# Two mixer blocks and their experts on one core: the token mixer's two branches in the other order, RWKV's two directions in turn, and eight extra weight slots for the first expert

## The chip, the core and the metric

The kernel runs on one core of a Trainium2 chip. TensorE (PE) multiplies matrices, VectorE (DVE), ScalarE (ACT) and GpSimd (POOL) do the elementwise work, and SyncE (SP) issues nearly all weight transfers. The metric is the device time of one execution in microseconds. Each engine runs its own instructions in order, so what stands in what place of an engine's row is a part of the design.

## What is computed

Two transformer blocks follow each other. The first has 16 meta tokens and 256 tokens (272 rows of 1024); the second works on the 256 tokens and on a context of 256.

```
# block 1
u    = rmsnorm(h);  rq, rk, rv, rg, mq, mk, mv, mo, gates = split(u @ w_in)
ret  = retention(rq, rk, rv), forward + backward;  y_ret = head_norm(ret) * silu(rg)
mq, mk = silu(conv5(mq, mk))
hm   = sigmoid(mo) * (mlstm(mq, mk, mv, gates), forward + backward);  y_m = head_norm(hm)
h   += concat(y_ret, y_m) @ w_out
aff  = softmax(rmsnorm(h) @ w_router);  16 experts take their 34 best tokens each
h   += sum over experts of  w_down(silu(w_gate x) * (w_up x)) * aff      # d_ff 2816
# block 2, on the tokens, with states that the context leaves
cols = u @ w_in_2;  o_a = gated_delta(cols_a), two directions;  o_b = rwkv7(cols_b), two directions
h   += merge(sigmoid gates, o_a, o_b) ;  h += two-level MoE(h), 32 experts
return rmsnorm(h)
```

Retention and mLSTM don't depend on one another; both go into the one product with `w_out`. The two directions of the RWKV scan don't depend on one another either; their results are added.

## The kernel before

**The head** (`head_body`, from L399) computes block 1's mixer. Every projection is a set of three fp32r products (`product3`, L299: high times high, high times low, low times high) whose weights come by `wgroup`. The order in which the code is written is: retention's q and k (`rqk`), retention's scores (`rs`), its values, its sums (`ro`, `head_norm`); then mLSTM's q and k, values and gates, its scores (`ms`, L616) and sums (`mo`, L639) head by head, each sum evicted through a small chain on ACT and DVE (`rc`, L642 to L647); then the output gate, a head norm (`y<-hnmv`, L733), and the projection `gate` of retention. Afterwards `y` is transposed in eight pieces k (`trb`, L680), four of retention (with `gate`, L684) and four of mLSTM, split into high and low parts, and multiplied with `w_out` (`pM`, L395, for the meta rows, then `wo`). Between these stand small steps of block 2's conditioning (`ada`). `route` then does the softmax and, in some 20 small steps on DVE, the choice of tokens (`af`, `wk`, `gt`, `eq`, `ce`).

**The experts** (`ffn`, L820). Weights arrive in slots of 1 MB, taken in turn (`Ring`) from three pools of ten slots together; for expert 0 a pool `rx` with four further slots stands on the right side of the memory, in the ring behind the ten. SP issues the transfers in one row (L241 for `w_gate` and `w_up`, L283 for `w_down`, L265 for the context's `w_in_2`), and each waits until the tiles that lay at its slot's place are done with. An expert's weights are 34.6 MB. `expert` (L883) computes gate and up products (`gu`, L901) and `second` (L917) the down product (`dn`, L933). From expert 1 on, the context's share of block 2 (`ctx_pre`) is placed between these products.

**RWKV** (L1414) takes its 8 heads in four pairs j. For each pair and each direction d there is a front (`rwkv_front`: products `rmt`, L1628), an inverse (`mixed_inverse`: many 32x32 products `r0ic`, `r1ic`, L1164, then `r1ib`, `r1iy`), and a scan of four steps (`rwkv_back`: `rp`). A step is a chain: `T` times state (L1661, which waits for the state `rSU`), copy on ACT, product with `Y` (L1676), copies on DVE and ACT, update (L1683), the new `rSU` on DVE (L1688); L1691 adds the step's output. Before, `rwkv_back` is run to its end for direction 0 and then for direction 1. The projections of what comes later (`pc`, L1102, and `gz`, L1836) are placed behind instructions of direction 0 (`hop`, `fill`). The delta-rule branch (`gic`, `gib`, `gp`) and these projections share the stretch with RWKV.

What sets the order: the code is written in one order, and a scheduler that plans with a timeline of its own then orders every engine's instructions; on the chip each engine runs them in that order and waits where an operand is missing.

Of the kernel before, what the change touches and what calls it, by code (L numbers as in the profile page):

```python
# [10 lines left out]
F32 = mybir.dt.float32  # L11
# [5 lines left out]
P = 128  # L17
D = 1024
KD = D // P
# [36 lines left out]
RX = 4  # L56
# [106 lines left out]
class Net:  # L163
# [237 lines left out]
    def head_body(self, W):  # L401
# [9 lines left out]
        wq = self.wgroup(w_in, 0)  # L411
# [6 lines left out]
        for q in (64, 96):  # L418
            nc.gpsimd.tensor_add(self.fold4, self.fold4, self.ident[:, q:q + NMETA])

# [21 lines left out]
        for hh in range(4):  # L442
            s = rvt(hh, f"strip{hh}")[:, :416] if hh < 3 else W.tile([P, 416], F32, name="strip3", tag="mv0", padded_shape=[P, 516])
# [13 lines left out]
        rqk = []  # L457
        for g in range(2):
            dst = W.tile([P, 4, NTOK], F32, name="qk", bufs=4)
            scale = (P ** -0.5) if g == 0 else 1.0  # L460
            for j in range(4):
                if j % 2 == 0:
                    w = wq if g + j == 0 else self.wgroup(w_in, 512 * g + 128 * j)
                    if g:
                        step(g)
                pj = projT(w, j % 2)
                raw = W.tile([P, NTOK], F32, name="raw", tag="raw", padded_shape=[P, NTOK + 4], bufs=3)
                nc.scalar.activation(raw, pj, AF.Copy, scale=scale)
                tmp = W.tile([P, NTOK], F32, name="rtmp", tag="rtmp", bufs=2)
                for i in (0, 64):  # L470
                    a, c = slice(i, i + 64), slice(64 - i, 128 - i)
                    nc.vector.scalar_tensor_tensor(tmp[a], pj[c], scale, self.ht("sin")[c], op0=ALU.mult, op1=ALU.mult)
                nc.gpsimd.tensor_mul(dst[:, j, :], raw, self.ht("cos"))
                nc.vector.tensor_add(dst[:, j, :], dst[:, j, :], tmp)
            rqk.append(dst)

        big = W.tile([P, 4, 3, NTOK], F32, name="pret", tag="big")
        prets = [big[:, hh] for hh in range(4)]
        self.ptag = "pc"
        for hh in range(4):  # L480
            pret = prets[hh]
            for t, (n0, n) in enumerate(TT):
                b = self.bank("rs")
                nc.tensor.matmul(b[:n, :NTOK], rqk[1][:, hh, n0:n0 + n], rqk[0][:, hh, :], start=True, stop=True)
                nc.vector.tensor_mul(pret[:n, t, :], b[:n, :NTOK], strip[hh][:n, 144 - n0:416 - n0])
# [3 lines left out]
        rv = [rvt(t, f"rv{t}") for t in range(3)]  # L489
# [24 lines left out]

        projN(1024, out_rv)


        self.ptag = "pc"
        for t, (n0, n) in enumerate(TT):
            ro = self.bank("ro")  # L520
            for hh in range(4):
                for m, (m0, mn) in enumerate(TT):
                    nc.tensor.matmul(ro[:n, hh * P:(hh + 1) * P], prets[hh][:mn, m, n0:n0 + n],
                                     rv[m][:mn, hh * P:(hh + 1) * P], start=(m == 0), stop=(m == 2))
            self.head_norm(W, y[:n, t, 0:512], ro[:n], n, f"r{t}")


        self.ptag = "pa"
        mqk = []
        for g in range(2):  # L530
            dst = W.tile([P, 4, NTOK], F32, name="qk", bufs=4)
            for j in range(4):
                if j % 2 == 0:
                    w = self.wgroup(w_in, 2048 + g * 512 + 128 * j)
                    step(1)
                pj = projT(w, j % 2)
                pad = W.tile([P, NTOK + 4], F32, name="pad", tag="raw", bufs=3)
# [1745 lines left out]
```

## Time and profile before

| | |
|---|---|
| median of 3 runs | 2490.26 us (2485.04 to 2493.68) |
| profiled execution | 2486.04 us |
| its span, first to last instruction | 2484.3 us |
| TensorE busy | 2306.2 us, 93% of the span |
| mean granted TensorE clock | 0.965 of full speed |
| VectorE, ScalarE, GpSimd busy | 40%, 26%, 14% |
| transferred | 755.06 MB, mean 304 GB/s |

The span falls into the head (0 to some 268 us), the routing (to 293 us), the sixteen experts (to some 1668 us), block 2's mixer (to some 2200 us) and its MoE. The profile shows for each engine what it did and what ended its idle time; a stretch's own numbers say more than the means of the span, since the stages have different limits.

### The profile page before, as it was taken

Reading aid. Unit: us, or ns where it says so; the run is one execution under the profiler, and the core shown is the slowest. Engines: PE = TensorE matmul, PEld = TensorE weight load, DVE = VectorE, ACT = ScalarE, POOL = GpSimd, SP = SyncE. Lnnn points to the kernel's source line nnn. Section 1 sums busy time; section 2 is a strip of 40 time slices with the busy share of each in tenths; the row PEclk is TensorE's granted clock in tenths of the full one; section 3 lists DMA queues with packets and bytes.
Section 4 is the critical chain, followed back from the end, with each engine's and each line's share of the span. In section 5 each row is a group of like instructions: output and inputs, shape, how many; then the busy total and the mean of one; then the engine's idle time right before and its main releaser. Section 6 shows DMA issues by size and latency. Waiting matters only on the chain. (4 is left out here: it accounts for less than half of the span.)

```text
span 2484.3 us, 45165 instructions
## 1 busy us (share of the span) xinstructions
PE 2306.2 (93%) x18736; PEld 1252.2 (50%) x18736; DVE 990.8 (40%) x2419; ACT 656.0 (26%) x1652; POOL 350.8 (14%) x627
## 2 busy tenths in 40 slices
PE   7997799999999999899999998978998999989997
PEld 6765433444444434333433333327777777865554
DVE  6655311323332133223133133216566563645545
ACT  4443111211211222111122121114534332522221
POOL 3101100000001111101011011004243231300000
PEclk9998899999999999999999999998997889999999
DMA  7664999999999999999999999992311113689995
GB/s 244 225 233 132 336 407 402 402 407 405 400 407 398 361 402 405 406 408 406 406 400 406 406 406 406 408 354 67 88 37 38 45 27 95 224 278 365 367 367 182
DMA packets 318816, 755.06 MB, mean 304 GB/s; under 512 B 12944, under 2 KB 158016, under 8 KB 315536
## 3 DMA queue, kind: packets, MB, share of 16 engines
q1 hardware_dynamic: 317104, 747.67, 80.3%
q0 software_dynamic: 1504, 4.46, 0.6%
q8 instruction: 150, 2.46, 0.4%
q14 instruction: 58, 0.48, 0.1%
HBM read 751.03 MB, written 1.05 MB: 303 GB/s over the span
## 5 line engine op out<-in xcount | busy, mean ns | idle before, releaser
L901 PE MATMUL gu<-w,xs 128*64 128x512 f32 (+1 forms) x3072 | 677.2, 568 | 24.3 <-DMA w<-in_w_up 17.2
L901 PEld LDWEIGHTS gu<-w,xs 128*64 128x64 f32 x3072 | 197.5, 137 | 325.2 <-issue 258.0
L933 PE MATMUL dn<-w,hT 128*64 128x512 f32 x1408 | 338.1, 604 | 17.0 <-DMA w<-in_w_down 16.9
L1102 PE MATMUL pc<-luT,w 128*128 128x256 f32 x688 | 177.5, 398 | 1.8 <-DMA w<-in_w_in 1.8
L933 PEld LDWEIGHTS dn<-w,hT 128*64 128x64 f32 x1408 | 88.4, 136 | 171.7 <-issue 116.7
L1102 PEld LDWEIGHTS pc<-luT,w 128*128 128x128 f32 x688 | 126.6, 195 | 19.2 <-DMA w<-in_w_in 2.0
L2139 PE MATMUL egu<-w,exs 128*64 128x256 f32 x1024 | 123.2, 383 | 0.0
L2139 PEld LDWEIGHTS egu<-w,exs 128*64 128x64 f32 x1024 | 74.6, 136 | 39.4 <-issue 6.9
L1672 POOL TENSOR_SCALAR rsw<-rSU,rwc 64x64 f32<-64x64 f32 x112 | 37.2, 332 | 389.3 <-DVE rSU L1688 379.0
L911 DVE TENSOR_TENSOR hid<-hid,gu 128x512 f32<-128x512 f32 (+1 forms) x48 | 30.8, 642 | 130.8 <-ACT hid L306 130.7
L912 DVE TENSOR_TENSOR hid<-hid,gu 128x512 f32<-128x512 f32 (+1 forms) x48 | 30.8, 642 | 119.3 <-PE gu L901 119.2
L1102 PE MATMUL pc<-cuT,w 128*128 128x256 f32 x288 | 71.1, 391 | 0.0
L304 ACT ACTIVATE hid<-gu 128x512 f32<-128x512 f32 (+1 forms) x48 | 26.9, 561 | 160.9 <-PE gu L901 160.7
L2166 PE MATMUL edn<-w,ehT 128*64 128x512 f32 x256 | 67.7, 597 | 0.7 <-ACT ehT L321 0.5
L1102 PEld LDWEIGHTS pc<-cuT,w 128*128 128x128 f32 x288 | 52.0, 189 | 30.8 <-issue 20.4
L1680 DVE COPY rSU<-rp 64x64 f32<-64x64 f32 x64 | 13.8, 215 | 133.0 <-PE rp L1676 132.7
L1628 PE MATMUL rmt<-rT,rBK 128*128 128x128 f32 (+1 forms) x256 | 54.4, 355 | 13.1 <-DVE rT L1615 6.2
L289 ACT CAST wp<-w 128x1024 fp32r<-128x1024 f32 (+1 forms) x48 | 55.1, 1188 | 40.3 <-DMA w<-in_w_in 22.6
L299 PE MATMUL pj<-uTh,wp 128*128 128x272 f32 x320 | 64.8, 296 | 0.0
L290 DVE TENSOR_TENSOR wp<-w,wp 128x1024 fp32r<-128x1024 f32 (+1 forms) x44 | 57.2, 1323 | 15.0 <-ACT wp L289 15.0
L1185 DVE TENSOR_TENSOR r0iB<-r0iB,r0ic 128x128 f32<-128x128 f32 x48 | 13.7, 285 | 114.2 <-PE r0ic L1164 107.4
L2182 DVE TENSOR_TENSOR acc<-acc,esc 128x512 f32<-128x512 f32 x64 | 41.0, 682 | 42.5 <-PE esc L2181 42.5
(675 smaller groups left out, 3560.1 us busy)
## 6 DMA issues: line engine op xcount, KB each, us to landing
w<-in_w_down SPq DMA_DIRECT2D x176, 1024.0 KB, 16.8
w<-in_w_gate SPq DMA_DIRECT2D x128, 1024.0 KB, 17.7
w<-in_w_up SPq DMA_DIRECT2D x128, 1024.0 KB, 17.5
w<-in_w_gate SPq DMA_DIRECT2D x64, 768.0 KB, 16.1
w<-in_w_up SPq DMA_DIRECT2D x64, 768.0 KB, 14.8
w<-in_moe_w_gate SPq DMA_DIRECT2D x32, 1024.0 KB, 13.2
w<-in_moe_w_up SPq DMA_DIRECT2D x32, 1024.0 KB, 12.2
w<-in_moe_w_down SPq DMA_DIRECT2D x32, 1024.0 KB, 11.3
```

The source lines that it names most:

```text
L289: self.nc.scalar.copy(hi, src)
L290: (eng or self.nc.vector).tensor_sub(lo, src, hi)
L299: self.nc.tensor.matmul(out, a[x], b[y], start=(i == 0 and x + y == 0), stop=(i == n - 1 and x == 1))
L901: ins = nc.tensor.matmul(b[h * 64:(h + 1) * 64, :w], xs[:, k, :], ws(k, slice(h * w, (h + 1) * w)), start=(k == 0), stop=(k == KD - 1))
L911: nc.vector.tensor_mul(hid, hid, gu[0][:, :w])
L933: ins = nc.tensor.matmul(dn[0][dc * 64:(dc + 1) * 64], hT[:, j, h * 64:(h + 1) * 64], wd(h * nf + j, slice(dc * 512, (dc + 1) * 512)), sta ...
L1102: self.nc.tensor.matmul(b, w(k), uT[:, k, :], start=(k == 0), stop=(k == KD - 1))
L1628: ins = nc.tensor.matmul(b[:, i], BK[:, c0 + i, h:h + 2, :], T[:, h, c0 + i, :, :], start=True, stop=True)
L1672: nc.gpsimd.tensor_scalar(sw[r], SU[r, h, c, :], wc[r, c:c + 1], 0.0, op0=ALU.mult, op1=ALU.add)
L2139: nc.tensor.matmul(b[64 * i:64 * i + 64, x * 256:x * 256 + 256], xs[:, k, i, :], w[i](k), start=(k == 0), stop=(k == KD - 1))
L2166: nc.tensor.matmul(b[64 * i:64 * i + 64, :], hT[:, j, 64 * i:64 * i + 64], wd[i](j, cs), start=(j == 0), stop=(j == 1))
L2182: nc.vector.tensor_add(h[:, t, cs], h[:, t, cs], b)
```

## The change

Three things are changed.

1. In the head the code for mLSTM's q and k, values, scores and sums stands first, and retention's q and k, scores, values and sums after it. The first weights fetched are those of columns 2048 on. The transposes run over k = 4 to 7 (mLSTM) and then 0 to 3 (retention). One small tile (`strip3`) gets a place of its own.
2. The pool `rx` of four slots becomes eight pools of one slot each, put into the ring in a given order. The routing's tiles no longer lie at the places of these slots: they are cut from the tile of the rotary table, which is done with by then, or are allocated early (`self.small`).
3. `in_turn` takes the `rwkv_back` of the two directions alternately, one piece (up to the next `yield`) of each.

```diff
-RX = 4
+RX = (2, 1, 0, 5), (3,), (6, 7, 4)
...
-        wq = self.wgroup(w_in, 0)
+        wq = self.wgroup(w_in, 2048)
...
+        self.small = dict(m8=W.tile([NE, 5, 8], F32, name="m8"), ng=W.tile([NE, 2], F32, name="ng"),
...
+        nc.gpsimd.memset(self.small["on"], 1.0)
...
-        rqk = []
-        for g in range(2):
...
-        projN(1024, out_rv)
...
-            self.head_norm(W, y[:n, t, 0:512], ro[:n], n, f"r{t}")
...
         sums(3, pm)
+        self.ptag = "pa"
+        rqk = []
+        for g in range(2):
...
+        rv.extend(rvt(t, f"rv{t}") for t in range(3))
+        projN(1024, out_rv)
...
+            self.head_norm(W, y[:n, t, 0:512], ro[:n], n, f"r{t}")
...
-        for k in range(KD):
+        for k in (4, 5, 6, 7, 0, 1, 2, 3):
...
-        lt = W.tile([P, NTOK], F32, name="lt", tag="raw", padded_shape=[P, NTOK + 4], bufs=3)
+        tmp = W.tile([P, HTAB_N], F32, name="rtab", tag="htab")[:, :5 * NTOK].rearrange("p (i t) -> p i t", i=5)
+        lt = tmp[:, 0, :]
...
-        af = W.tile([NE, NTOK], F32, name="af", tag="fr")
-        wk = W.tile([NE, NTOK], F32, name="wk", tag="lf")
+        af, wk, gt, eq = (tmp[:NE, i, :] for i in range(1, 5))
...
-            with self.tc.tile_pool(name="rx", bufs=RX, side="right", reuse_waits="tile") as rx:
-                self.rings = Ring(rings + [rx] * RX)
+            with ExitStack() as ex:
+                rx = [ex.enter_context(self.tc.tile_pool(name=f"rx{i}", bufs=1, side="right", reuse_waits="tile"))
+                      for i in range(sum(map(len, RX)))]
+                early, mid, last = ([rx[i] for i in part] for part in RX)
+                self.rings = Ring(rings + early + mid + last)
...
-            ys = []
-            for d in range(2):
-                ys.append(run(self.rwkv_back(j, d, x, fr[d], env)))
+            ys = self.in_turn(tags, [self.rwkv_back(j, d, x, fr[d], env) for d in range(2)])
...
+    def in_turn(self, tags, gens):
+
+        out = [None] * len(gens)
+        todo = list(range(len(gens)))
+        while todo:
+            for i in list(todo):
+                self.ptag = tags[i]
+                try:
+                    next(gens[i])
+                except StopIteration as end:
+                    out[i] = end.value
+                    todo.remove(i)
+        return out
```

How this moves instructions shows in the engines' rows. First TensorE at the end of the head, before:

```order
L639 MATMUL mo<-mv_567,pm_1634 128x129
L639 MATMUL mo<-mv_568,pm_1644 128x129
L639 MATMUL mo<-mv_568,pm_1648 128x129
L680 MATMUL trb<-ctab,y 128x16 x3
L680 MATMUL trb<-ctab,y 128x128 x6
L680 MATMUL trb<-ctab,y 128x16
L680 MATMUL trb<-ctab,y 128x128 x2
L395 MATMUL pM<-w,um 32x256 x8
```

The same place now; ahead of this piece, back to the last projection (`pj`, of retention's gate), stand only transposes and eight `ada`:

```order
L689 MATMUL trb<-ctab,y 128x16
L689 MATMUL trb<-ctab,y 128x128 x2
L1045 MATMUL ada<-w,adas 32x512 x4
L1034 MATMUL ada<-ctab,arow 128x128 x4
L396 MATMUL pM<-w,um 32x256 x8
L300 MATMUL wo<-wp,yT_2134 128x256 x2
```

The mLSTM sums, which stood last before the transposes, now stand in mid-head, the last two heads' 24 in one run; this is its end on TensorE, with retention's scores (`rs`) and projections of its values (`pn`) behind it:

```order
L604 MATMUL mo<-mv_592,pm_1000 128x129
L604 MATMUL mo<-mv_593,pm_1010 128x129
L604 MATMUL mo<-mv_594,pm_1020 128x129
L604 MATMUL mo<-mv_594,pm_1024 128x129
L648 MATMUL rs<-qk 16x272
L648 MATMUL rs<-qk 128x272 x2
L648 MATMUL rs<-qk 16x272
L648 MATMUL rs<-qk 128x272
```

So between the last projection and `w_out` only transposes and `ada` are left on TensorE.

Next SP's row of transfers for expert 0, before (each is 1 MB into one slot; numbers tell the slots' tiles apart):

```order
L241 DMA w_2736<-in_w_gate 128x2x1024
L241 DMA w_2762<-in_w_up 128x2x1024
L241 DMA w_2764<-in_w_up 128x2x1024
L265 DMA w_3004<-in_w_in_2 128x8x256
L265 DMA w_3395<-in_w_in_2 128x8x256
L241 DMA w_2766<-in_w_up 128x2x1024
L241 DMA w_2768<-in_w_up 128x2x1024
L283 DMA w_2795<-in_w_down 128x2x1024
```

and now:

```order
L242 DMA w_2752<-in_w_gate 128x2x1024
L242 DMA w_2778<-in_w_up 128x2x1024
L242 DMA w_2780<-in_w_up 128x2x1024
L242 DMA w_2782<-in_w_up 128x2x1024
L242 DMA w_2784<-in_w_up 128x2x1024
L284 DMA w_2809<-in_w_down 128x2x1024
```

The two loads of `w_in_2` for the context have left this place; they now stand thirty rows further on, behind the last weights of expert 0 and ten transfers of expert 1.

Last TensorE in the RWKV scans of the last pair of heads, before: the end of direction 0's scan, with direction 1's inverse and the projections around it (tiles of direction 0 and 1 have 0 and 1 in their names).

```order
L1668 MATMUL rp13_15082<-rSU0_14709,rT0_11729 64x64 x2
L1676 MATMUL rp24_15090<-rP0_15086,rY0_14801 64x64 x2
L1102 MATMUL pc_15070<-luT_11623,w_11668 128x256 x4
L1164 MATMUL r1ic_15221<-r1iB_15100 32x32 x9
L1691 MATMUL rp13_15082<-rSU0_14709,rMR0_14719 64x64 x2
```

Some fifteen rows later direction 1's scan begins. Now the two stand in one another:

```order
L1681 MATMUL rp13_15208<-rSU1_14779,rT1_11753 64x64 x2
L1703 MATMUL rp24_15265<-rSU0_14732,rKt0_14741 64x64 x2
L1110 MATMUL pc_15189<-luT_11646,w_11691 128x256
L1711 MATMUL rp13_15246<-rSU0_14732,rMR0_14742 64x64 x2
L1172 MATMUL gic_16148<-giZ_16014,giB_16013 32x32
L1172 MATMUL gic_16171<-giB_16074 32x32 x9
L1688 MATMUL rp13_15208<-rSU1_14779,rT1_11753 64x64 x2
L1696 MATMUL rp24_15229<-rP1_15222,rY1_14856 64x64 x2
L1681 MATMUL rp13_15293<-rSU0_14732,rT0_11752 64x64 x2
```

A step of one direction is now followed by a step of the other, and direction 1 ends one to two steps behind direction 0 instead of a whole scan behind.

## Rows read from the trace of the kernel before

**Rows 1.** The page: busy time of each engine (PEld: TensorE's weight loads).

```profile
PE 2306.2 (93%) x18736; PEld 1252.2 (50%) x18736; DVE 990.8 (40%) x2419; ACT 656.0 (26%) x1652; POOL 350.8 (14%) x627
```

**Rows 2.** Busy time by stretch: length, engines, granted clock, DMA share, GB/s.

```profile
175.00:200.00 25.00, 25.00 (x175) 17.42 (x174) 13.14 (x33) 13.74 (x33) 0.23 (x1) 1.00 0.80 285
200.00:225.00 25.00, 14.28 (x76) 9.53 (x75) 16.96 (x65) 9.36 (x25) 5.93 (x7) 0.70 0.29 87
```

**Rows 3.** TensorE's waits, 198 to 232 us: total us, times, longest.

```profile
PE trb L680 <- DVE y L733: 5.5, 3, 2.9
```

**Rows 4.** TensorE in order of time, 196 to 232 us: start, us, instruction.

```profile
197.49 0.49 PE L299 MATMUL pj<-uTh,wp 128*128 128x272 f32 x1
...
225.76 0.90 PE L680 MATMUL trb<-ctab,y 128*128 128x128 f32 x3 [1.04 <-DVE y L733]
227.32 0.90 PE L680 MATMUL trb<-ctab,y 16*128 16x16 f32 x3 [0.67 <-DVE yT L689]
229.87 1.94 PE L395 MATMUL pM<-w,um 128*32 128x256 f32 x16 [1.65 <-POOL um L690]
```

**Rows 5.** TensorE's groups, 198 to 232 us: busy us, mean ns, idle before.

```profile
L639 PE MATMUL mo<-mv,pm 128*128 128x129 f32 (+3 forms) x48 | 9.6, 344 | 5.3 <-DVE rc L643 4.5 <-DVE y L647 0.8
```

**Rows 6.** SP's waits before transfers, 264 to 300 us: total us, times, longest.

```profile
SPq L241 <- DVE eq L798: 10.4, 1, 10.4
```

**Rows 7.** Transfer rate, 180 to 420 us, in 40 slices of 6 us.

```profile
GB/s 201 365 288 189 169 11 0 0 27 147 178 233 300 373 255 363 253 221 402 364 407 412 400 399 405 410 410 408 408 411 408 411 408 408 408 371 405 400 396 407
```

**Rows 8.** TensorE's waits, 293 to 450 us.

```profile
PE dn L933 <- DMA w<-in_w_down: 2.6, 5, 0.6
PE gu L901 <- DMA w<-in_w_gate: 2.4, 3, 1.1
```

**Rows 9.** Busy time by stretch among the experts, columns as in rows 2.

```profile
450.00:700.00 250.00, 247.57 (x1902) 107.19 (x1900) 82.04 (x189) 55.09 (x125) 21.55 (x28) 1.00 1.03 403
...
975.00:1300.00 325.00, 304.56 (x2380) 119.61 (x2378) 86.28 (x204) 60.72 (x146) 36.95 (x82) 0.99 1.03 405
```

**Rows 10.** TensorE in order of time, 355 to 372 us, columns as in rows 4.

```profile
368.53 0.41 PE L973 MATMUL ebs<-crw,mcol 128*128 128x36 f32 x2
```

**Rows 11.** Busy time by stretch in RWKV, columns as in rows 2.

```profile
1897.00:1988.00 91.00, 85.53 (x1210) 70.20 (x1210) 44.46 (x138) 30.95 (x100) 27.50 (x57) 0.78 0.14 37
1988.00:2057.00 69.00, 62.42 (x901) 48.03 (x900) 44.11 (x132) 24.29 (x82) 25.37 (x44) 0.85 0.09 25
2057.00:2098.00 41.00, 41.00 (x728) 32.98 (x727) 13.91 (x36) 14.44 (x44) 6.09 (x11) 1.00 0.27 70
```

**Rows 12.** Steps of the scans on TensorE in order of time.

```profile
1823.47 0.56 PE L1661 MATMUL rp<-rSU,rT 128*64 128x64 f32 x4 [1.01 <-DVE rSU L1688]
...
1827.98 0.34 PE L1661 MATMUL rp<-rSU,rT 128*64 128x64 f32 x4
...
1900.74 0.34 PE L1661 MATMUL rp<-rSU,rT 128*64 128x64 f32 x4
...
1927.92 0.47 PE L1691 MATMUL rp<-rSU,rMR 128*64 128x64 f32 x2
...
1951.38 0.34 PE L1661 MATMUL rp<-rSU,rT 128*64 128x64 f32 x4
...
1988.05 0.33 PE L1691 MATMUL rp<-rSU,rMR 128*64 128x64 f32 x2
...
2030.45 0.34 PE L1661 MATMUL rp<-rSU,rT 128*64 128x64 f32 x4
...
2057.74 0.34 PE L1691 MATMUL rp<-rSU,rMR 128*64 128x64 f32 x4
...
2097.40 0.34 PE L1691 MATMUL rp<-rSU,rMR 128*64 128x64 f32 x4
```

**Rows 13.** TensorE's waits, 1715 to 2107 us.

```profile
PE rp L1661 <- DVE rSU L1688: 11.1, 6, 4.3
PE rmt L1628 <- ACT rT L1617: 4.4, 1, 4.4
```

More of the change, by code (lines that the diff above doesn't have):

```diff
@@ L419, in head_body @@
             nc.gpsimd.tensor_add(self.fold4, self.fold4, self.ident[:, q:q + NMETA])
+        self.small = dict(m8=W.tile([NE, 5, 8], F32, name="m8"), ng=W.tile([NE, 2], F32, name="ng"),
+                          sm=[W.tile([P, 3], F32, name=f"sm{t}") for t in range(3)],
+                          ss=[W.tile([P, 2], F32, name=f"ssb{t}") for t in range(3)],
+                          on=W.tile([NE, NTOK], F32, name="on"))
+        nc.gpsimd.memset(self.small["on"], 1.0)
         xn = self.norm_rows(W, h, "a")
@@ L473, in head_body @@
[L473 to L485, printed above, removed]
+                pad = W.tile([P, NTOK + 4], F32, name="pad", tag="raw", bufs=3)
@@ new lines, in head_body @@
+                nc.gpsimd.memset(pad[:, 0:2], 0.0)
+                nc.gpsimd.memset(pad[:, NTOK + 2:], 0.0)
+                nc.scalar.copy(pad[:, 2:NTOK + 2], pj)
+                c = 4 * g + j
+                tmp = W.tile([P, NTOK], F32, name="cv", tag="rtmp", bufs=2)
+                nc.vector.tensor_scalar(tmp, pad[:, 0:NTOK], self.pc("conv_w", c * 5), self.pc("conv_b", c),
+                                        op0=ALU.mult, op1=ALU.add)
+                for k in range(1, 5):
+                    nc.vector.scalar_tensor_tensor(tmp, pad[:, k:k + NTOK], self.pc("conv_w", c * 5 + k), tmp,
+                                                   op0=ALU.mult, op1=ALU.add)
@@ L488, in head_body @@
+                self.sigmoid(dst[:, j, :], tmp)
+                nc.gpsimd.tensor_mul(dst[:, j, :], dst[:, j, :], tmp)
+            mqk.append(dst)
         self.y = y = self.pers.tile([P, 3, D], F32, name="y", tag="tok")
-        rv = [rvt(t, f"rv{t}") for t in range(3)]
+        rv = []
         mv = [W.tile([P, 4, 129], F32, name=f"mv{t}") for t in range(3)]
@@ L513, in out_mo @@
             self.sigmoid(mo[t][:n, c * 256:c * 256 + 256], b)
-        projN(1024, out_rv)
[L518 to L524, printed above, removed]
-            self.head_norm(W, y[:n, t, 0:512], ro[:n], n, f"r{t}")
-        self.ptag = "pa"
-        mqk = []
-        for g in range(2):
[L531 to L537, printed above, removed]
-                nc.gpsimd.memset(pad[:, 0:2], 0.0)
-                nc.gpsimd.memset(pad[:, NTOK + 2:], 0.0)
-                nc.scalar.copy(pad[:, 2:NTOK + 2], pj)
-                c = 4 * g + j
-                tmp = W.tile([P, NTOK], F32, name="cv", tag="rtmp", bufs=2)
-                nc.vector.tensor_scalar(tmp, pad[:, 0:NTOK], self.pc("conv_w", c * 5), self.pc("conv_b", c),
-                                        op0=ALU.mult, op1=ALU.add)
-                for k in range(1, 5):
-                    nc.vector.scalar_tensor_tensor(tmp, pad[:, k:k + NTOK], self.pc("conv_w", c * 5 + k), tmp,
-                                                   op0=ALU.mult, op1=ALU.add)
-                self.sigmoid(dst[:, j, :], tmp)
-                nc.gpsimd.tensor_mul(dst[:, j, :], dst[:, j, :], tmp)
-            mqk.append(dst)
         for name in ("rp", "rn"):
@@ L775, in route @@
             nc.gpsimd.tensor_scalar(self.un[:n, t, :], h[t][:n], rs[t], 0.0, op0=ALU.mult, op1=ALU.add)
[L776 to L778 removed]
+        af, wk, gt, eq = (tmp[:NE, i, :] for i in range(1, 5))
+        m8, ng, on = (self.small[name] for name in ("m8", "ng", "on"))
         nc.scalar.copy(af, aT[:NE, :NTOK])
```

65 lines of the change are left out of this document (43 added, 22 removed).

## Prediction

> **What bounds the kernel now.** The page comes first, and it warns: TensorE is busy for 93% of the span, its weight loads for half of it [rows 1]. The profile only models where a matmul ends, so 93% does not mean that nothing is to be had; each stage has to be asked for itself. So I read busy time by stretch, then in each stretch the waits, then single instructions in order of time.
>
> In the head TensorE is full until 198 us and then falls to 14.28 of 25 us, with the granted clock at 0.70 in the mean, between its levels of 2.4 and 1.2 GHz, after TensorE had begun to wait [rows 2]. The last projection starts at 197.49 and the first product with `w_out` at 229.87 [rows 4]: 32 us in which the mLSTM sums, their eviction chain, a head norm and 24 transposes come one after the other. The waits there end on DVE: 5.5 us for the head norm [rows 3], 5.3 us of the sums for their own chain [rows 5].
>
> Before the first expert the transfers have a hole: 255, 363, 253, 221, 402, 364 GB/s in the six slices from 264 to 300 us against 408 later [rows 7], and SP stood for 10.4 us before one transfer until the routing's `eq` was done with [rows 6]. Among the experts the limit changes hands. From 293 to 450 us TensorE waits 5.0 us for weights [rows 8]; from 450 to 700 it is busy 247.57 of 250 us, with the transfers close behind at 403 GB/s; from 975 on it is idle some 20 of 325 us at 405 GB/s, thus bound by transfers [rows 9].
>
> In RWKV a pair's chain of direction 0 (front, inverse, four steps) sets the pace. Its four steps took 36.7 us for pair 2 and 27.3 us for pair 3 [rows 12], 32.0 in the mean, 8.0 us a step, while direction 1's inverse ran beside them. Direction 1's scan of a pair runs beside the next pair's front and inverse (1900.74 to 1927.92) [rows 12]. Only after the last pair is it alone behind direction 0: 2057.74 to 2097.40, 40 us [rows 12].
>
> **The mixer's order.** Nothing is added or removed; 48 sums and the scores leave the tail for the dense part. What stays between the last projection and `w_out` is one sigmoid, four gated transposes with their splits, `ada` and the chain to `um`. I estimate 11 us: the last transposes of before followed each other after 1.56 us (225.76 and 227.32), four of them make 6.2; from the last to the first product with `w_out` it took 2.55 us [rows 4]; and 2 us for evicting the gate, which no row shows alone, between 0 and the 4.5 us for which a sum waited for its chain [rows 5]. The tail shrinks from 32.4 to 11, 21 us. The moved sums cost in their new place 9.6 us of TensorE if their waits vanish, and 14.9 with the 5.3 us of waits [rows 5], which is possible since the last two heads' 24 sums still stand in one run. 21 less 9.6 to 14.9 gives 6 to 11; I take 8. The ends: 0, if the scores' chains also hold up projections in the dense part, and 21, if the sums fit wholly into gaps that busy time hides there. The head norm's 5.5 us [rows 3] go in any case, because it now runs while retention is projected. The late part of the head then ends on the gate's eviction on ACT and DVE. The new first weights (columns 2048 on) are as large as the old, and `on`'s memset and the other early tiles lie on engines that wait there for the first loads: 0.
>
> **The slots.** SP no longer waits for `eq`, and eight slots can fill while the routing works. The hole of 264 to 300 us is worth 3.5 MB, the six differences to 408 GB/s times 6 us, thus 8.7 us of transfer; the two slices behind the wait for `eq` (253 and 221) alone 2.05 MB or 5.0 us [rows 7]. The routing itself is unchanged, so TensorE starts expert 0 no sooner. Earlier weights can only remove waits for weights before the stretch that TensorE bounds: 5.0 us [rows 8]. Behind it the transfers again follow TensorE's release of slots. I take 5, between 0 (the waits come back as others) and 8.7. The two context loads and the small GpSimd loads move behind expert 0's weights. Behind them on SP stand weights of expert 1 that need slots which TensorE frees at about the same time. The router's columns are first used at 368.53 [rows 10], the context's first projections after that. They still wait for nothing later than down products of expert 0, which end ahead of that: 0. If they came late, TensorE would stand at `ebs`, in order; the nearest rows are its waits for weights there, 5.0 us [rows 8].
>
> **RWKV in turn.** The products are the same in number. In the tail of the last pair, direction 1's scan no longer follows direction 0's. But the 41 us are no empty time: TensorE shows 41.00 busy, of it 32.98 under weight loads [rows 11], since projections and the delta rule's inverses fill them, and this work remains. What is surely free is 8 us. In the earlier pairs direction 1's scan no longer disturbs the next pair's front and inverse. TensorE's visible waits that end on scan state or on tiles that both share are 11.1 and 4.4 us, 15.5 together [rows 13]; half of them, 8 us, I count as gone, as the alternating scans will have waits too. That assumes that a pair of steps, one of each direction, takes the 8.0 us that a step of direction 0 took beside an inverse. Sum 16 us. The lower end: a step alone took 4.5 us (1823.47 to 1827.98), one beside a front 6.8 us (27.2 over four) [rows 12]; one after the other they make 11.3, 3.3 us over 8.0, times 16 steps 53, less the 8 from the tail: 45 us lost. The upper end: besides 8 and 15.5, the tail's work could move into the stretch before it, which has 69 less 48.03, 21 us, without weight loads [rows 11]: 45 us won.
>
> One rule speaks against more. The trace shows weight loads over 80% of 2057 to 2098 and 70% of 1988 to 2057 [rows 11]. The Trainium skill (Perfetto Trace Analysis, Identifying the Most-Contended Engine) calls matmul busy time a bad measure and takes weight-load busy time as the better one. By that rule the last stretch gives up 8 us and no more, and the one before it has little room; by the busy time of the matmuls alone it would give up nothing. The trace has no stretch that decides between the two; it only shows both numbers.
>
> **The sum.** 8 + 5 + 16 = 29 us. The profiled execution took 2486.04 us (span 2484.3 and 1.7 around it), so 2457; it lies 4.2 us under the median of 2490.26, so against the median 2461.
>
> **Rivals.** Prices are against the median.
>
> A. RWKV gains nothing: the work that filled direction 1's last scan is merely done later. For it: 33 of 41 us under weight loads, and the delta rule's chain still follows. Against it: the low clock of 0.78 and 0.85 before 2057 [rows 11] shows TensorE at 1.2 GHz for a part of it, after work in which it had much to wait for. 2490 − 13 = 2477.
>
> B. RWKV gains the upper end, since two independent chains fill each other's waits: 2490 − 8 − 5 − 45 = 2432. For it: weight loads leave 21 us free before the tail. Against it: DVE was already 44.11 of 69 us busy there [rows 11], and both directions now want it at once.
>
> C. Slower: the alternation couples the two chains. TensorE, DVE and ACT keep to their order, so a late `rSU` of one direction holds the other's step, which stands behind it. With 11.3 us for a pair of steps RWKV loses 45, and the time is 2490 − 13 + 45 = 2522. It decides from the point at which a pair takes 8.0 + (13 + 8)/16 = 9.3 us; below that the whole is still faster than before. For it: 4.3 us was the longest single wait for `rSU` [rows 13]. Against it: a chain alone needed 4.5 us a step, so 8.0 hold more than one and a half of them, and most of a step is waiting for copies in which the other can compute.
>
> D. The order does not do in the head what it should: the sums' waits move with them and the scores stall projections, so that part gives 0, and RWKV gives 0 too. Only the slots' 5 us remain: 2485, which cannot be told from no change.
>
> **How the numbers follow.** The forecast (2447 to 2473) has 0.48, A 0.22, B 0.14, C 0.07, D 0.09. A measurement of this kernel can tell about 0.3%, 7.5 us, from no change. Faster by more: the forecast, A (13 us, with a margin of 6) and B, 0.84, of which some 0.02 lie too near: 0.82. Within: D and those, 0.11. Slower: C, 0.07. The range leaves out C and the half of B that lies beyond its price, some of D too: 2425 to 2484.
>
> **What would show it.** Right: the last projection of the head and the first `w_out` product 11 us apart instead of 32; no wait on the routing's tiles before SP's transfers, and TensorE without waits for `w_gate` between 293 and 450 us; the last `rp` less than 10 us behind the last of direction 0; a pair of steps at 8 us. Wrong: waits of `mo` or of projections in mid-head as long as those that left the tail; pairs of steps over 9.3 us; direction 1's projections piled up after the last `rp`, with the end of the delta rule as late as before. A routing that itself gets slower through its new tiles would also make the prediction wrong.

## The result and the profile after

The changed kernel takes 2459.06 us in the median (2458.13 to 2465.39, four runs), the kernel before 2489.46 on the same chips (2485.04 to 2493.68); the ratio is 0.9877, with a 95% interval of 0.9861 to 0.9893. That is 30 us less, where 29 were forecast. The parts of the sum didn't come out like their total: the head and the slots gave less, the stretch of RWKV gave more, and what it gave beyond the forecast is no more than another order of the same instructions moves.

First the page of the changed kernel, the row that answers to [rows 1]. TensorE has the same number of instructions and 25 us less of busy time.

```profile
span 2457.4 us, 45180 instructions
## 1 busy us (share of the span) xinstructions
PE 2280.8 (93%) x18736; PEld 1238.1 (50%) x18736; DVE 979.8 (40%) x2419; ACT 652.7 (27%) x1652; POOL 353.7 (14%) x627
```

The stages are found by single instructions of TensorE in order of time (start, us, instruction). The head's last projection and the first product with `w_out`, the rows that answer to [rows 4]:

```profile
215.75 0.28 PE L300 MATMUL pj<-uTh,wp 128*128 128x272 f32 x1
...
227.91 0.85 PE L396 MATMUL pM<-w,um 128*32 128x256 f32 x12
```

The tail is 12.2 us long, where 11 were estimated, against 32.4 before. But the last projection comes 18 us later than before, so that the first product with `w_out` comes only 2 us sooner. Why shows in mid-head, by stretch (length, TensorE, weight loads, VectorE, ScalarE, GpSimd, granted clock, DMA share, GB/s) and by the sums that waited there:

```profile
125.00:150.00 25.00, 18.83 (x111) 11.49 (x110) 10.96 (x33) 8.03 (x20) 1.09 (x2) 0.80 0.45 155
150.00:175.00 25.00, 24.48 (x142) 16.54 (x140) 7.02 (x18) 2.05 (x6) 0.00 (x0) 0.86 0.12 43
```

```profile
141.19 4.32 PE L604 MATMUL mo<-mv,pm 16*16 16x129 f32 x16 [3.36 <-DVE y L612]
...
148.32 2.38 PE L604 MATMUL mo<-mv,pm 16*128 16x129 f32 x8 [2.81 <-DVE y L612]
```

The run of 24 sums waits as long as the sums in the old tail did, 6.2 us here against 5.3 [rows 5], but now all of it for `y`, where it was mostly `rc`; and the granted clock is low behind these waits, as it was in the old tail [rows 2].

Ahead of the experts the slots and the moved routing tiles do what they should: SP no longer stands for the routing's `eq` [rows 6] (of the routing it waits 2.6 us for the logits), and from 264 to 300 us 12.95 MB come in where 11.14 came before. In the 60 us after that, fewer come in. These are the totals of the two stretches, 264 to 300 and 300 to 360 us, of the changed kernel; in the second, GpSimd's own transfers (q0) have appeared:

```profile
DMA packets 3383, 12.95 MB, mean 360 GB/s; under 512 B 192, under 2 KB 192, under 8 KB 3381
```

```profile
DMA packets 6768, 23.98 MB, mean 400 GB/s; under 512 B 428, under 2 KB 444, under 8 KB 6766
...
q0 software_dynamic: 352, 1.20, 5.7%
```

and the same two stretches of the kernel before, with GpSimd's transfers in the first:

```profile
DMA packets 4457, 11.14 MB, mean 309 GB/s; under 512 B 193, under 2 KB 2257, under 8 KB 4455
...
q0 software_dynamic: 352, 1.20, 10.4%
```

```profile
DMA packets 6869, 24.41 MB, mean 407 GB/s; under 512 B 404, under 2 KB 404, under 8 KB 6867
```

Up to 430 us, the end of expert 1, the changed kernel has 1.91 MB more, as the totals of that stretch show, the kernel before first:

```profile
DMA packets 46382, 120.95 MB, mean 281 GB/s; under 512 B 2081, under 2 KB 24769, under 8 KB 43282
```

```profile
DMA packets 46877, 122.86 MB, mean 286 GB/s; under 512 B 2109, under 2 KB 24797, under 8 KB 43777
```

TensorE's waits for weights from 289 to 450 us, which answer to [rows 8], are no shorter: 6.3 us together against 5.0.

```profile
PE dn L941 <- DMA w<-in_w_down: 2.8, 6, 0.6
PE gu L909 <- DMA w<-in_w_up: 2.2, 2, 1.6
PE gu L909 <- DMA w<-in_w_gate: 1.3, 2, 0.7
```

In RWKV the two scans of the last pair now run in one another. The first and the last steps of direction 0 (2014.96, 2039.61) and direction 1 (2026.37, 2054.60), and the first `got`, with which the delta rule ends, in TensorE's order of time, as in [rows 12]:

```profile
2014.96 0.34 PE L1681 MATMUL rp<-rSU,rT 128*64 128x64 f32 x4
...
2026.37 0.34 PE L1681 MATMUL rp<-rSU,rT 128*64 128x64 f32 x4
...
2039.61 0.34 PE L1711 MATMUL rp<-rSU,rMR 128*64 128x64 f32 x4
...
2054.60 0.34 PE L1711 MATMUL rp<-rSU,rMR 128*64 128x64 f32 x4
...
2103.54 0.56 PE L1877 MATMUL got<-ctab,tail 128*128 128x128 f32 x2 [0.27 <-DVE tail L1872]
```

Direction 1 ends 15 us behind direction 0, against 40 before [rows 12]. Measured from there the first `got` comes 49 us later; before it was 34 us (2097.40 to 2131.43). So 15 of the 43 us by which the last step came sooner are given back by work that had filled the old scan. By stretch, which answers to [rows 11]:

```profile
1890.00:1965.00 75.00, 70.34 (x1222) 59.67 (x1221) 50.78 (x155) 31.66 (x105) 32.53 (x60) 0.91 0.17 46
1965.00:2055.00 90.00, 79.53 (x1472) 62.08 (x1474) 49.15 (x154) 32.11 (x111) 28.44 (x53) 0.92 0.16 42
2055.00:2104.00 49.00, 47.27 (x332) 41.33 (x327) 21.85 (x51) 21.16 (x56) 6.72 (x11) 1.00 0.47 143
```

The granted clock is 0.91 and 0.92 where it was 0.78 and 0.85 [rows 11], between 2.4 and 1.2 GHz. In the two stretches ahead of these, from the first pair on, it is lower than before, 0.86 and 0.90 against 0.91 and 0.95. TensorE's waits of `rp` for scan state have hardly shrunk, 11.3 us against 13.8 (the 11.1 of [rows 13], and 2.7 at L1691):

```profile
PE rp L1711 <- DVE rSU L1700: 5.9, 6, 2.3
PE rp L1681 <- DVE rSU L1708: 5.4, 4, 2.1
PE rmt L1648 <- ACT rT L1637: 4.4, 1, 4.4
```

One measure serves in all that follows: the mixer stretch, from the start of the last `dn` group of the experts to the start of the first `mo` of the merge. Before, it is 1666.96 to 2140.38; after, 1663.92 to 2112.49. In the table it is taken from the last single `dn`, 1.3 us later: 472.1 and 447.2 us. So 24.9 of the 26.9 us between the two profiled spans lie there, 3.0 lie ahead of it, and 1 is given back behind it.

Over the mixer stretch TensorE is idle as long as before, 44.8 us against 44.4. What went is busy time, 25 us of it, for the same instructions and at nearly the same granted clock; the kernel before first:

```profile
1668.30:2140.38 472.08, 427.70 (x5384) 343.78 (x5381) 273.55 (x754) 199.90 (x602) 152.17 (x281) 0.90 0.23 63
```

```profile
1665.26:2112.49 447.23, 402.47 (x5385) 329.07 (x5381) 267.51 (x754) 198.93 (x602) 153.34 (x281) 0.91 0.24 66
```

### The profile page after: what moved, and what is told of

It reads as the page before. It is cut to its first block, busy times and chain, and to the rows that moved or that the text cites. A ratio compares the mean times of both kernels' runs of the same rounds, so it can differ in the third digit from the quotient of the medians.

```text
span 2457.4 us, 45180 instructions
## 1 busy us (share of the span) xinstructions
PE 2280.8 (93%) x18736; PEld 1238.1 (50%) x18736; DVE 979.8 (40%) x2419; ACT 652.7 (27%) x1652; POOL 353.7 (14%) x627
## 5 line engine op out<-in xcount | busy, mean ns | idle before, releaser
L305 ACT ACTIVATE hid<-gu 128x512 f32<-128x512 f32 (+1 forms) x48 | 26.9, 560 | 163.6 <-PE gu L909 163.4
L1110 PEld LDWEIGHTS pc<-cuT,w 128*128 128x128 f32 x288 | 52.1, 190 | 30.8 <-issue 20.4
L958 DVE SCALAR_TENSOR_TENSOR acc<-sc,aff,acc 128x512 f32<-128x512 f32 x64 | 43.7, 744 | 37.9 <-PE sc L956 37.7
## 6 DMA issues: line engine op xcount, KB each, us to landing
w<-in_w_gate SPq DMA_DIRECT2D x128, 1024.0 KB, 17.6
w<-in_w_up SPq DMA_DIRECT2D x64, 768.0 KB, 14.9
w<-in_moe_w_down SPq DMA_DIRECT2D x32, 1024.0 KB, 11.3
```

The lines of the kernel that those rows point to most:

```text
L958: nc.vector.scalar_tensor_tensor(dst, b, self.aff[:, t + 1, e:e + 1], dst, op0=ALU.mult, op1=ALU.add)
L1110: self.nc.tensor.matmul(b, w(k), uT[:, k, :], start=(k == 0), stop=(k == KD - 1))
```

## First experiments: each part alone

Theory from the two traces: RWKV brings some 24, the head 4, the slots nothing. Rival: the forecast's own sum, 16, 8 and 5.

**The turns alone** (`t1_turn`), in the kernel before:

```diff
-            ys = []
-            for d in range(2):
-                ys.append(run(self.rwkv_back(j, d, x, fr[d], env)))
+            ys = self.in_turn(tags, [self.rwkv_back(j, d, x, fr[d], env) for d in range(2)])
```

> The kernel before with the two RWKV directions in turn and nothing else. Theory from the two traces: RWKV carries nearly all of the gain (the products after it end 24 us earlier relative to its start), so 24 us less than before, about 2466, ratio 0.990. Rival, the sum of the forecast: 16 us less, about 2474, ratio 0.9935, and the rest of the gain is in the head and the slots.

Measured: 2463.85 us, ratio 0.9890 (0.9866 to 0.9913); the mixer stretch 451.9. That is 27 us less than before, nearer to the theory's 24 than to the rival's 16.

**The mixer's order alone** (`t2_order`): the moved blocks and the order of the transposes, four slots and the routing's tiles as before.

```diff
-        wq = self.wgroup(w_in, 0)
+        wq = self.wgroup(w_in, 2048)
...
-        for k in range(KD):
+        for k in (4, 5, 6, 7, 0, 1, 2, 3):
```

> The kernel before with the mixer's new order and nothing else (four extra slots, routing tiles as before). Theory: the first expert's product starts some 4 us earlier and 3 to 4 us arrive at the end, about 2486, ratio 0.9985; the wait of the mLSTM sums shows in mid-head. Rival, the sum of the forecast: 8 us, about 2482, ratio 0.997.

Measured: 2472.70 us, ratio 0.9926 (0.9908 to 0.9944). 18 us less, which neither side had expected. And they are not in the head. The first product of expert 0 starts at 292.3 us (293.5 before), and the experts end where they did; the mixer stretch alone, in which not a line was changed, is 13 us shorter. Its last `dn` group and the first `mo` of the merge:

```profile
1667.16 1.94 PE L936 MATMUL dn<-w,hT 128*64 128x512 f32 x8 [0.65 <-DMA w<-in_w_down]
...
2127.57 1.64 PE L300 MATMUL mo<-mob,wp 128*128 128x256 f32 x11
```

The engines' rows tell why it can be so: the planner has put the RWKV stretch in another order. Of the 5380 TensorE instructions that the traces show between the experts and the merge, 2512 places, from the second pair of heads on, hold another operation, tile or shape than in the kernel before, although the code there is the same.

**The slots alone** (`t3_slots`), and **order and slots without turns** (`t4_order_slots`):

```diff
-RX = 4
+RX = (2, 1, 0, 5), (3,), (6, 7, 4)
...
-        af = W.tile([NE, NTOK], F32, name="af", tag="fr")
-        wk = W.tile([NE, NTOK], F32, name="wk", tag="lf")
+        af, wk, gt, eq = (tmp[:NE, i, :] for i in range(1, 5))
```

> The kernel before with eight extra slots and the routing's tiles moved, and nothing else. Theory: the transfers before expert 0 grow by 2 to 3 MB, but they take the place of the context's loads, which then run in the full stream, so 0 to 1 us, about 2489.5, ratio 0.9995 to 1. Rival, the sum of the forecast: 5 us, about 2485, ratio 0.998.

> The changed kernel with the two RWKV directions run one after the other as before. Theory: what the head and the slots bring together is what the trace shows at the end of the experts, 3 us, about 2487, ratio 0.9988. Rival, the sum of the forecast: 13 us, about 2477, ratio 0.995.

Measured: the slots alone 2487.85 us, ratio 0.9986 (0.9972 to 1.0000), which lies between the two numbers and tells nothing apart; order and slots 2467.99, ratio 0.9906 (0.9886 to 0.9926), 19 us below what was expected of it, because its mixer stretch is the one of the order alone, row by row, and takes 458.6 us against 459.1. It is 4.7 us faster than the order alone (2461.21 to 2469.83 against 2469.93 to 2474.64, six runs each). The parts don't add up: 27, 18 and 3 alone, 30 together.

## Second experiments: is it the planner's order?

If the order of the stretch is an answer of the planner to anything ahead of it, then an edit that does nothing for the head should move the time too. The smallest one is the order of the eight transposes at the head's end.

```diff
-        for k in range(KD):
+        for k in (4, 5, 6, 7, 0, 1, 2, 3):
```

in the kernel before (`u1_k_only`); with the new mixer order, the transposes set back to 0 to 7 (`u2_order_knat`); in the kernel before again, but

```diff
-        for k in range(KD):
+        for k in (0, 1, 2, 3, 7, 6, 5, 4):
```

(`u3_k5`); and the changed kernel with 0 to 7 (`u4_after_knat`).

> The kernel before with the eight transposes at the end of the head in the changed kernel's order (4 to 7, 0 to 3), and nothing else. The planner answers with another order of the RWKV stretch, 1700 us later. Theory: the 18 us that the new mixer order brought alone are such another order of that stretch, not the head; then this kernel, whose head is as before, also moves by several us between the end of the experts and the merge (472 us there before), to somewhere between 450 and 475 us, and the head ends within 2 us of before. Rival: the head itself brought them; then this kernel stays at about 2490, and 472 us in that stretch.

> The new mixer order, but the transposes over k = 0 to 7. Its RWKV stretch is ordered row by row as in the kernel with the transposes' order alone; only the head differs between the two. Theory: it differs from that kernel by the head alone, 0 to 4 us less. Rival, the mixer order is worth the 18 us that it brought alone: 18 us less than that kernel.

> The kernel before with the transposes over k = 0, 1, 2, 3, 7, 6, 5, 4. Rows of all engines in the head and the experts are as before but for the k in the transposes; the planner orders the RWKV stretch in yet another way. Theory: the stretch from the experts' end to the merge, 472 us before, comes out anywhere between 450 and 480. Rival: it stays within 3 us of 472, and the total within 7 us of before.

> The changed kernel, but with the transposes over k = 0 to 7. Theory: with the directions in turn the stretch from the experts' end to the merge takes 447 to 455 us in whatever order the planner finds (447 in the changed kernel, 452 with the directions in turn alone), so 2459 to 2467. Rival: the changed kernel's order is a lucky one, and this one gives back 15 us or more, 2474 or above.

Measured: `u3_k5` 2477.55 us, ratio 0.9947 (0.9928 to 0.9967): 12 us less than before from reversing four transposes. Its head ends where it did (expert 0 starts at 293.5 us in both), and all of the gain is in the mixer stretch, 462.1 us. The same two rows of it:

```profile
1666.49 1.94 PE L933 MATMUL dn<-w,hT 128*64 128x512 f32 x8 [0.66 <-DMA w<-in_w_down]
...
2129.91 1.30 PE L299 MATMUL mo<-mob,wp 128*128 128x256 f32 x9
```

`u1_k_only` 2484.29 us (0.9976, 0.9962 to 0.9990) and `u2_order_knat` 2482.90 (0.9964, 0.9948 to 0.9981) share one order of the stretch and differ by 1.4 us, within their intervals: so the mixer order itself is not worth the 18 us that came with it. `u4_after_knat` 2464.28 (0.9891, 0.9872 to 0.9910), with 454.4 us in the stretch: with turns another order costs 5 us and not 15. The theory holds on all four, but for the head of `u1_k_only`, which ends 2.8 us later instead of within 2. `w2_turn_k` below, which also transposes mLSTM first where its sums still come last, starts expert 0 as late (296.2).

## Third experiments: slots, and the wait in mid-head

**Four PSUM banks for the mid-head sums** (`w1_bank`), in the changed kernel:

```diff
-            self.ptag = "pc"
+            self.ptag = "pm" if hh == 3 else "pc"
```

**Turns with the transposes' order, no more** (`w2_turn_k`), which has the same order of the stretch as `w1_bank`; and **four extra slots instead of eight** (`w3_four_slots`), with the stretch of the changed kernel:

```diff
-RX = (2, 1, 0, 5), (3,), (6, 7, 4)
+RX = (2, 1, 0), (3,), ()
```

> The changed kernel, with the last head's mLSTM sums in the two other PSUM banks, so that the 24 sums in mid-head have four banks instead of two and those of two heads can run in one another. Theory: the 6.2 us of waits of the sums in mid-head and the low clock behind them (0.51 and 0.64 from 140 to 160 us) go, so the first expert starts 5 to 8 us sooner than in the changed kernel (289.4 there), and some of that arrives at the end, 2453 to 2458 if the planner's order of the RWKV stretch (another one again) is no worse. Rival: the sums wait for the eviction chain itself and not for a bank; then the first expert starts within 2 us of 289.4.

> The kernel before with the directions in turn and the transposes in the changed kernel's order; mixer order and slots as before. Its RWKV stretch is ordered row by row as in the kernel with four PSUM banks for the sums. Theory: the stretch from the experts' end to the merge takes 447 to 455 us as in the other three kernels with the directions in turn, and 462 to 472 in those without; the total is 6 to 12 us above the kernel with four banks, by the head and the slots. Rival: the spread of the planner's orders (459 to 473 us without turns) is as wide with turns, and it comes out above 458.

> The changed kernel with four extra slots instead of eight, the routing's tiles still clear of them; mixer, RWKV and all other rows unchanged. Theory from the traces: the end of the experts stays within 1.5 us, since what eight slots fetch early takes the place of the context's loads, 2458 to 2461. Rival from the medians of the runs with and without the slots: 3.5 to 4.7 us slower, 2463.

Measured: `w1_bank` 2462.40 us (0.9889, 0.9871 to 0.9908); expert 0 starts at 289.9, within 1 us of the changed kernel, as the rival had it. The sums still wait 4.4 us at one place, and what VectorE waits for from 130 to 152 us shows that the number of banks is not the root of it:

```profile
DVE rc L608 <- ACT rc L607: 5.4, 3, 3.0
DVE wp L291 <- ACT wp L290: 4.4, 2, 4.1
```

The sums' eviction (`y`, L612) stands behind a split of projection weights (`wp`), and that waits for ScalarE's half of the split, which waits for the weights. The low clock stays too, 0.59 from 140 to 150 us against 0.51 in the changed kernel. There the same chain can be followed from ScalarE's wait, 130 to 152 us,

```profile
ACT wp L290 <- DMA w<-in_w_in: 3.6, 2, 2.8
```

to its start on SP, 105 to 135 us: the weights' transfers (L384) stand behind loads of the conditioning (`in_ada_w`, L1020), and these wait for a slot. One of the weights' transfers itself stood 9.7 us for a slot that `pM` held.

```profile
SPq L1020 <- PE ada L1045: 24.0, 4, 12.0
SPq L384 <- PE pM L396: 9.7, 1, 9.7
```

`w2_turn_k` took 2472.05 us (0.9933, 0.9918 to 0.9947), 457.2 in the stretch: between the theory's 455 and the rival's 458, thus undecided by itself. It is 9.7 us above `w1_bank`, the size that was expected but not the place: by the profiles 3.6 us lie at the end of the experts and 6.0 in a stretch that is ordered alike. `w3_four_slots` took 2457.45 us (0.9875, 0.9858 to 0.9891) against 2459.06 for the changed kernel: four slots are not slower than eight. It is the lowest median of all, but not by more than its interval.

**Few ada loads** (`x1_few_ada`), to see what the wait in mid-head is worth:

```diff
-ADA_COUNT = [1] * 6 + [2] * 20
+ADA_COUNT = [3] * 2 + [0] * 20
...
         for c, k in ADA_STEPS:
+            if 0 < k < 7:
+                continue
```

> The changed kernel, which leaves out 18 of the 24 steps of block 2's conditioning (the ada loads and products for rows 128 to 895 of each third) and does the other six first, so that no ada load stands among the projections' weights on SP in mid-head; the 24 mLSTM sums still stand in one run. The products left out, 120 of 168 ahead of the head's last projection, are worth 16 us of TensorE at 0.133 us each, so without any other effect that projection starts at 199.8 instead of 215.75. Theory: in mid-head the sums' evictions on ACT and DVE stand behind weight splits whose weights are late because SP waits with an ada load ahead of them; then the 6.2 us of waits of the sums and the low clock of 140 to 160 us go too, and the projection starts 8 us or more sooner than 199.8. Rival: the sums wait for their own eviction chain or their two banks; then 5 us or more of waits of the sums remain and it starts within 3 us of 199.8.

Measured: the waits of the sums are nearly gone, as the theory said. Of all waits of TensorE from 100 to 200 us these are left at the sums:

```profile
PE mo L604 <- DVE pm L590: 0.8, 1, 0.8
...
PE mo L604 <- DVE rc L608: 0.6, 1, 0.6
```

But the last projection starts at 201.5 us, not sooner than the 199.8 that the missing products alone account for. The time went into the clock: with hardly a wait, 125 to 150 us was granted 0.50, that is 1.2 GHz throughout. It fell at 125 us, at two short waits of the sums, 0.75 and 0.57 us; this is the first, with the last sums at the full clock:

```profile
122.43 2.42 PE L604 MATMUL mo<-mv,pm 16*16 16x129 f32 x16 [0.75 <-DVE pm L590]
```

```profile
125.00:150.00 25.00, 23.40 (x71) 14.05 (x72) 10.70 (x41) 6.20 (x21) 1.09 (x2) 0.50 0.02 3
```

So the visible wait goes when the ada loads go, and in this kernel that gave nothing. The loads went together with their products on TensorE, whose end they wait for, so the two are not told apart. Two waits for split weights, 1.9 us together, came in ahead of 62 us. Why the clock is lowered during these sums is not settled.

The whole took 2464.81 us, in one run, beside one run of the kernel before with 2480.34. With less work in the head the totals can't be compared; but the mixer stretch holds all of its instructions, in a fifth order with turns, and took 461.6 us.

## What each part is worth

All profiled runs side by side, in us; "order" names equal orders of the mixer stretch.

| kernel | turns | order | expert 0 starts | experts end | mixer stretch | median |
|---|---|---|---|---|---|---|
| before | no | a | 293.5 | 1668.3 | 472.1 | 2489.5 |
| t3_slots | no | a | 293.5 | 1670.8 | 473.5 | 2487.9 |
| t2_order | no | b | 292.3 | 1668.5 | 459.1 | 2472.7 |
| t4_order_slots | no | b | 289.6 | 1662.8 | 458.6 | 2468.0 |
| u1_k_only | no | c | 296.3 | 1670.8 | 464.9 | 2484.3 |
| u2_order_knat | no | c | 289.7 | 1666.3 | 472.1 | 2482.9 |
| u3_k5 | no | d | 293.5 | 1667.8 | 462.1 | 2477.6 |
| after | yes | e | 289.4 | 1665.3 | 447.2 | 2459.1 |
| w3_four_slots | yes | e | 290.6 | 1664.9 | 441.4 | 2457.5 |
| t1_turn | yes | f | 292.1 | 1667.4 | 451.9 | 2463.9 |
| u4_after_knat | yes | g | 290.5 | 1667.4 | 454.4 | 2464.3 |
| w1_bank | yes | h | 289.9 | 1666.5 | 451.2 | 2462.4 |
| w2_turn_k | yes | h | 296.2 | 1670.1 | 457.2 | 2472.1 |
| x1_few_ada (less work in the head) | yes | i | 280.3 | 1656.7 | 461.6 | 2464.8 (one run) |

The stretch of the same order differs by up to 7 us between two kernels (c, e, h), so a difference of a few us in a single profile says nothing. The mean of the four orders without turns is 465.6 us, of the five with turns 453.3 (451.2 without `x1_few_ada`). **The turns are worth about 12 us**, but the orders lie 14 us apart without turns and 17 with them, so that so few of them leave some 10 us open on either side; and they overlap, since `x1_few_ada` took longer than order b. The kernel before had the slowest of the orders without turns, the changed kernel the fastest with them; the other 13 us or so of the 25 in the stretch are such a draw.

What the turns do in every order shows at two groups of products. Over the mixer stretch TensorE is busy at `rp` for 44.8 to 48.6 us in the six kernels with turns and `x1_few_ada`, and for 50.6 to 54.7 us in the seven without; at `r1ic` for 17.6 to 19.0 and for 20.4 to 22.7 us. By the means of the orders that is 9 us less for both together. Before, `rp` and then `r1ic`:

```profile
1668.30:2140.38 472.08, 54.24 (x608) 35.13 (x608) 20.31 (x80) 20.02 (x96) 0.90 0.23 63
1668.30:2140.38 472.08, 22.71 (x1024) 15.42 (x1024) 4.56 (x16) 4.22 (x16) 0.90 0.23 63
```

and after:

```profile
1665.26:2112.49 447.23, 45.52 (x608) 31.59 (x608) 19.98 (x80) 19.59 (x96) 0.91 0.24 66
1665.26:2112.49 447.23, 17.83 (x1024) 13.22 (x1024) 4.56 (x16) 4.16 (x16) 0.91 0.24 66
```

So with turns the same products hold TensorE for less time. Why, and how much of it is the clock, was not tried.

**The head**: the seven kernels with the new mixer order start expert 0 at 290.3 us in the mean, the four with the old one and retention transposed first at 293.2, and the experts end at 1666.0 against 1668.6. So 3 us, where `t1_turn` and the kernel before, with the same head, are 1.4 us apart. **The slots**: in the profiles with the new mixer order the experts end at 1665.5 us with eight slots (four kernels) and at 1666.6 with four (three kernels), with a spread of 5 us among the first; that tells nothing. The medians say more. Two pairs with the same order of the stretch, without and with the slots and the moved routing tiles, are 3.5 us (before and `t3_slots`) and 4.7 us (`t2_order` and `t4_order_slots`) apart; but `w3_four_slots`, which has the moved tiles and four slots, is no slower than eight. So four more slots gave nothing in the one pair that tells, and what clearing the routing's tiles gives lies somewhere from 0 to 5 us; it was not tried alone.

## Why the prediction was right, point by point

**The total** was 29 us forecast and 30 measured, and the direction and the range hold. The sum hit because two errors offset each other: by the two profiles the head and the slots were put 10 us too high, the mixer stretch 9 too low. Some 13 us of that stretch are a draw of the order, of which the text knew nothing, so that 29 and 30 lie so close is luck.

**The mixer's order, 8 us forecast, 3 measured.** The tail's term was right (11 us estimated, 12.2 measured). The step that was mis-sized is the price of the moved sums: "9.6 us of TensorE if their waits vanish, and 14.9 with the 5.3 us of waits", of which the middle was taken. They wait 6.2 us in their new place, and from 140 to 155 us TensorE's 10.5 us of work there ran at a granted clock of 0.50 or 0.51, by an estimate from these numbers 5 us longer than at the full clock; the last projection came 18 us later. The 3 us lie below the range given, 6 to 11, and above its outer end 0. The text's own sign of being wrong, waits of `mo` in mid-head as long as those that left the tail, has come, and with it nearly what rival D says of the head. The reason that the text named, the 24 sums in one run, is the place; the cause of the waits is one link further on, the weights behind the ada loads; and where these waits are gone, in `x1_few_ada`, the clock takes the time.

**The slots, 5 us forecast, 0 to 5 measured.** The hole in the transfers was read rightly: 1.8 MB more come in from 264 to 300 us. What fell short is the other side of it: "The two context loads and the small GpSimd loads move behind expert 0's weights", priced at 0. GpSimd's 1.2 MB lay in the hole before, and the two loads of `w_in_2` were issued late in it, from 285.48 us. Moved, they run in the full stream, 400 GB/s from 300 to 360 us, and in these two profiles the experts' start is fed no better: TensorE waited 6.3 us there instead of 5.0, 1.3 of it for `w_gate`, where none was forecast. The account up to 430 us, when expert 1 is nearly done, is 1.91 MB more than before, 4.7 us at 408 GB/s; but in this kernel the head, and with it all of the stream, is 4.1 us earlier, and little is left for the slots. The 3.5 and 4.7 us of the medians stand against that reading, and what they come from is open. A hole that other bytes already fill in part is not worth its full width. The trace of before had the row for it, the GpSimd transfers of 264 to 300 us, and the sum left it out.

**RWKV in turn, 16 us forecast, about 12 measured as a mean over orders, with some 10 open on either side, and 25 in this one.** The tail gave what rival A feared in part: the first `got` comes 49 us after the last step instead of 34. The premise that a pair of steps takes 8.0 us was nearly met: the four pairs of scans of direction 0 took about 37, 29, 26 and 25 us, 7.4 a step. So C didn't come, although the first pair, with 9.3 us a step, stands just at its bound. "The last `rp` less than 10 us behind the last of direction 0" was wrong (15). The step that the runs don't bear out is the other half of the term, 8 us for half of the visible waits: those for scan state have hardly shrunk, the 4.4 us of `rmt` are as before, and TensorE's idle time in the whole stretch is the same. What went is busy time; most of the gain lies in pair 2, at a better clock: front and inverse took 54 us before and 46 after, its scan 37 and 26. With every order that has turns, `rp` and `r1ic` take less of TensorE's time. The term was about right in size, but not by its working.

**The rule of the Trainium skill** (Perfetto Trace Analysis, Identifying the Most-Contended Engine) was taken as a reason against more than 8 us in the last stretch. The share of weight loads there is 41.33 of 49 us now, 84% against 80%. No run decides between the two measures in the last stretch. The whole gained more than that stretch could give, because most of the gain came from before it; over the mixer stretch the share of weight loads was 73% and is 74%, and 25 us went all the same.

**What the text did not see** is that an edit in the head re-orders a stretch 1700 us later. It priced each part as if it moved its own stretch alone; the rows of the changed kernel showed the new order of RWKV, and it was put down to the turns. `u3_k5` shows that four transposes in reverse are enough, for 12 us.

## What to carry to other kernels

Where a planner orders the instructions, an edit is two edits: what it does, and a new draw of everything behind it. Before a gain is credited to the edit, look in which stage it lies, and set another kernel beside it whose edit is idle but whose order is new; where the draws differ by 10 us, effects of 5 need several draws on each side. When transfers are moved into a hole, count what already lies in it. And look at busy time as well as at waits: here the idle time of the mixer stretch stayed as it was, and its gain lay in the time that the same products took.

## What the runs showed of the hardware that was not expected

In `x1_few_ada` a stretch of TensorE with almost no waits (23.40 of 25 us busy) was granted half of the full clock, 0.50, and a run of 48 small products of 129 columns took 13.20 us there without a wait, 0.28 us each:

```profile
131.63 13.20 PE L604 MATMUL mo<-mv,pm 16*16 16x129 f32 x48
```

In the changed kernel 16 of them at the full clock took 2.63 us, 0.16 us each:

```profile
135.21 2.63 PE L604 MATMUL mo<-mv,pm 16*128 16x129 f32 x16
```

Before, the clock had fallen behind long waits, in the tail [rows 2] and, in the changed kernel's mid-head, behind one of 3.4 us; that had been read as cause and effect. In `x1_few_ada` it fell at waits of 0.75 and 0.57 us, and stayed low for 25 us in which TensorE was almost always busy.

The same products can take less of TensorE's time in another order: 427.70 us of busy time became 402.47 over the mixer stretch, with the idle time unchanged. And two kernels with equal orders of that stretch took 464.9 and 472.1 us there, 441.4 and 447.2, and 451.2 and 457.2: a fixed order leaves some 7 us open.
